# Reading PSUM banks with ScalarE first: a reordering of evacuations in a hybrid encoder trunk

## The chip, the core and the metric

One core of a Trainium2 chip runs the whole trunk as one program. Its engines are TensorE (PE, with its weight loads as PEld), VectorE (DVE), ScalarE (ACT), GpSimd (POOL) and SyncE (SP, which issues most DMAs). The metric is device time in microseconds; three runs of the kernel before give a median of 1218.54 us (1218.52 to 1218.98). The profiled execution took 1217.77 us.

## The reference, cut to what matters

```
for each of 2 layers:                      # 16 meta tokens + 1024 tokens, width 1024
  h = rms_norm(x, gain)
  f_in | q | k | v | gate = h @ w_in       # widths 512 each, gate 1024
  f_out = Re(DFT2(f_in over positions, group channels)) @ w_f       # 4 groups of 128
  q, k = rotary(rms_norm(q)), rotary(rms_norm(k))                   # 4 heads x 2 x 64
  o = (softmax(q1 k1) - lambda softmax(q2 k2)) @ v ; o = rms_norm(o)
  x = x + (concat(f_out, o) * silu(gate)) @ w_out
return x[meta tokens dropped]
```

## The kernel before

Positions lie in eight tiles of 128 tokens and a ninth of the 16 meta rows (`t == NT`). All is fp32: a matmul operand is split into a high part, rounded by ScalarE, and a low part (value minus high), mostly by VectorE, and a product is three matmuls (high x high, high x low, low x high).

A layer runs the Fourier groups first, then the projection of head 0 (`head_projection`), then `attention`. Attention is the main thread, over heads, groups of two tiles, and tiles. Between its steps it calls `fill`, which advances a generator of other TensorE work: the projections of heads 1 to 3, the output product of the Fourier half (`out_fourier`), that of the attention half (`phase_out`), and the next layer's norms.

The eight banks of PSUM are shared out in three pools. `big()` is one tile of three banks (S) for the scores; `gbank()` gives one of two banks (G) for projections and output products; `bank()` gives one of three banks (M) for transposes, for the product with V and for the Fourier maps. A bank is taken over by its next tile once every reader of the old one is done.

Within a bank the framework orders any two instructions of different engines after each other as they are written, reads too. So where the code writes a ScalarE read, a VectorE read and a ScalarE read of one bank, the third waits for the second, and the second for the first. These places matter here:

- `evacuate` (L467 to L487) empties a projection's bank: tanh of the gate (L482, ACT), gate product (L483, DVE), copy of q and k (L484), their squares (L486) and the copy of v (L487), all ACT. For the meta rows two parts are first summed from two row ranges of the bank: copy (L475, ACT) and add (L476, DVE), for each part in turn.
- `build_keys` (L576) transposes three tiles into an M bank and, for each half of the partitions, writes the scaled high part (L591, ACT) and the low part (L592, DVE).
- `build_queries` (L609) does the same with L621 (ACT) and L623 (DVE), and copies the high part to the other half of the partitions (L622, DVE; SBUF to SBUF).
- `out_tile` (L270) adds a G bank to the residual (L293, DVE); the meta rows have a second range of rows, copied by ACT (L296).
- `phase_out` (L773) prepares a tile by four transposes into a G bank (L786 to L788), read by L792 (ACT) and L793 (DVE).

`transposes` (L657) turns the softmax difference p into `ath` (L669, ACT) and `atl` (L670, DVE) over two M banks, and takes a third for the meta columns (L672). `scores` (L627) fills S (L636, L638), which one VectorE instruction (L643) empties.

The order on each engine is not written by hand. A list scheduler takes instructions by priority and by its own account of when each could start; `tc.high_priority(EVAC)` lifts evacuations, and `issue_after` holds filler behind marks in the attention. Each engine then runs its list strictly in order. The casts of the next weights (L182 ACT, L184 POOL or DVE) stand in the same lists.

Of the kernel before, what the change touches and what calls it, by code (L numbers as in the profile page):

```python
# [18 lines left out]
P = 128  # L19
# [31 lines left out]
def trunk(ctx: ExitStack, tc, x, meta, ngain, w_in, w_f, qg, kg, lq1, lk1, lq2, lk2, subg, w_out,  # L51
# [28 lines left out]
    def f(ap):  # L80
        return ap.bitcast(F32)
# [188 lines left out]
    def out_tile(yh, yl, wh, wl, xt, spare, t, wide, final=False):  # L270
# [10 lines left out]
        for group in groups:  # L281
# [8 lines left out]
            for (n, c, e), pb in zip(group, ps):  # L290
                o = xt[0:R, 512 * n + c:512 * n + e]
                with tc.high_priority(EVAC):
                    dve.tensor_tensor(o, o, pb[0:R, 0:e - c], op=ALU.add)  # L293
                    if t == NT:
                        low = spare[0:R].rearrange("p a b -> p (a b)")
                        act.copy(low, pb[2 * NMETA:2 * NMETA + R])  # L296
                        dve.tensor_tensor(o, o, low, op=ALU.add)
                if final:
                    sp.dma_start(out[0, P * t:P * t + P, 512 * n + c:512 * n + e], o)
                yield  # L300
# [156 lines left out]
    def head_projection(li, h, hT, hM, ep, wk, store, w, nxt, progress):  # L457
# [9 lines left out]
        def evacuate(t, ps, a, kv):  # L467
            nonlocal ss
            R = tile_rows(t)
            with tc.high_priority(EVAC):  # L470
                if t == NT:
                    pm = [ep.tile([P, 256], F32, tag="sq", name=nm("pm"), bufs=3) for _ in range(2)]
                    for part, u, v in ((pm[0], a, 256), (pm[1], 256, 384 if kv else 512)):
                        part = part[0:R, u % 256:(v - 1) % 256 + 1]
                        act.copy(part, ps[32:32 + R, u:v])  # L475
                        dve.tensor_tensor(part, ps[0:R, u:v], part, op=ALU.add)  # L476
                    pqk, pvg = pm[0], pm[1]
                else:
                    pqk, pvg = ps[:, 0:256], ps[:, 256:512]
                if not kv:  # L480
                    gs = ep.tile([P, P], F32, tag="gs", name=nm("gs"), bufs=2)
                    act.activation(gs[0:R], pvg[0:R, P:2 * P], AF.Tanh, scale=0.5)  # L482
                    dve.scalar_tensor_tensor(gs[0:R], gs[0:R], 1.0, pvg[0:R, P:2 * P], op0=ALU.add, op1=ALU.mult)  # L483
                act.copy(qk[0:R, t, a:256], pqk[0:R, a:256])  # L484
                sq = ep.tile([P, 256], F32, tag="sq", name=nm("sq"), bufs=3)
                act.activation(sq[0:R, a:256], pqk[0:R, a:256], AF.Square)  # L486
                act.copy(va[0:R, t, :], pvg[0:R, 0:P])  # L487
            if not kv:
                sp.dma_start(gtd[li][h][t, 0:R, :], gs[0:R])
# [67 lines left out]
    def attention(li, wk, store, fill, marks, ready, progress):  # L557
        ath = wk.tile([P, NT, 272], F32R, name="ath", bufs=1)
        atl = wk.tile([P, NT, 272], F32R, name="atl", bufs=1)
        att = wk.tile([80, 272], F32R, name="att", bufs=1)  # L560
        vt = wk.tile([80, P], F32R, name="vt", bufs=1)
        pool.memset(f(vt), 0.0)
        pool.memset(f(att), 0.0)
# [12 lines left out]
        def build_keys(h, upto, most=3):  # L576
# [3 lines left out]
            while upto > built.get(h, 0) and most > 0:  # L580
# [5 lines left out]
                for t in tiles:  # L586
                    R = tile_rows(t)
                    pe.transpose(pb[:, w:w + R], qk[0:R, t, P:256], ident[0:R, 0:R])
                    w += R
                for dst, s, o in zip(keys[h], half, half[::-1]):  # L590
                    act.activation(dst[s, a:a + w], pb[s, 0:w], AF.Copy, scale=kgc[s, li:li + 1])  # L591
                    dve.scalar_tensor_tensor(dst[o, a:a + w], pb[s, 0:w], kgc[s, li:li + 1], f(dst[s, a:a + w]),  # L592
# [4 lines left out]
        def build_values(h):  # L597
            va = store[h][1]
            vh = wk.tile([P, NT, P], F32R, tag="vh", name=nm("vh"), bufs=1)
            vl = wk.tile([P, NT, P], F32R, tag="vl", name=nm("vl"), bufs=1)  # L600
            act.copy(vh, va[:, 0:NT])
# [7 lines left out]
        def build_queries(h, gi):  # L609
# [9 lines left out]
            low = qlow[gi % 2]  # L619
            for dst, ql, s, o in ((qa, low[0], half[0], half[1]), (qb, low[1], half[1], half[0])):  # L620
                act.activation(dst[s, 0:w], pb[s, 0:w], AF.Copy, scale=qgc[s, li:li + 1])  # L621
                dve.tensor_copy(dst[o, 0:w], f(dst[s, 0:w]))  # L622
                dve.scalar_tensor_tensor(ql[s, 0:w], pb[s, 0:w], qgc[s, li:li + 1], f(dst[s, 0:w]),  # L623
                                         op0=ALU.mult, op1=ALU.subtract)
            return (qa, qb), low

# [52 lines left out]
        def values(vals, w):  # L679
# [5 lines left out]
            pe.matmul(po[:, 0:w], lhsT=vt, rhs=att[:, 0:w], start=False, stop=True)  # L685
            osb = wk.tile([P, 272], F32, tag="osb", name=nm("osb"), bufs=1)
            act.copy(osb[:, 0:w], po[:, 0:w])
            return osb

        def finish(h, gi, osb, ls):  # L690
            sets = [(0, 2, P)] + ([(2, 1, NMETA)] if len(group_tiles(gi)) > 2 else [])
            for i0, n, R in sets:
                t0 = group_tiles(gi)[i0]
                gt = wk.tile([P, 2, P], F32, tag="gt", name=nm("gt"), bufs=1)
                sp.dma_start(gt[0:R, 0:n], gtd[li][h][t0:t0 + n, 0:R, :].rearrange("t p d -> p t d"))
# [7 lines left out]
                so = sm.tile([P, 2], F32, tag="so", name=nm("so"), bufs=2)  # L703
                sqo = wk.tile([P, P], F32, tag="sqo", name=nm("sqo"), bufs=1)
                for i in range(n):
# [67 lines left out]
    def phase_out(li, nh, gb, wk, w, load, ready):  # L773
# [4 lines left out]
        def prepare(t):  # L778
# [5 lines left out]
            if t < NT and ("gy", li) in dbg:  # L784
                sp.dma_start(dbg["gy", li][:, t], ya.rearrange("p h d -> p (h d)"))
            pb = gbank()  # L786
            for k in range(4):
# [216 lines left out]
```

## Time and profile before

| | us |
|---|---|
| median of three runs | 1218.54 |
| profiled execution | 1217.77 |
| its span (first to last instruction) | 1216.0 |
| PE busy | 1164.0 (96%) |
| DVE busy | 835.8 (69%) |
| ACT busy | 643.1 (53%) |
| POOL busy | 264.7 (22%) |

The busy time of PE holds the time in which matmuls overlap or run slowly, so it says little of how full PE is; waits and the spacing of matmuls say more. The granted TensorE clock is 0.994 of full speed over the whole span. The first scores of layer 1 start at 215.9 us, those of layer 2 at 826.5 us.

### The profile page before, as it was taken

What the parts mean: (1) busy time and instruction counts of PE and PEld (TensorE: products, weight loads), DVE (VectorE), ACT (ScalarE), POOL (GpSimd) and SP (SyncE); (2) the same over time, 40 slices, a digit from 0 to 9 for tenths busy, and PEclk for the clock granted to TensorE, in tenths of its full rate; (3) what the DMA queues carried; (4) which work ended last, traced back from release to release, by engine and by line L of the source; (5) the groups of instructions that cost most, each with busy time, mean ns of one, the idle gap of its engine ahead of it and who ended that gap; (6) DMA issues with size and microseconds to landing.
All of it is one profiled execution on the core that took longest, in us unless ns stands there. A gap on an engine that the chain in (4) does not pass through costs nothing. (4 is left out here: it accounts for less than half of the span.)

```text
span 1216.0 us, 18757 instructions
## 1 busy us (share of the span) xinstructions
PE 1164.0 (96%) x6676; PEld 999.7 (82%) x6676; DVE 835.8 (69%) x1785; ACT 643.1 (53%) x1580; POOL 264.7 (22%) x239
## 2 busy tenths in 40 slices
PE   6999999999999999999999999999999999999998
PEld 5999886787787787788879999877888888878886
DVE  6352645777788788888684334458788888888963
ACT  6332324567666667566453223345576676756631
POOL 5111326023211212012012103160142122301200
PEclk9999999999999999999999999999999999999999
DMA  7420303003002004643436202120020110365353
GB/s 229 140 70 18 92 28 100 7 14 94 12 24 77 16 25 153 193 160 133 149 107 192 70 18 71 45 82 26 18 83 25 45 54 27 119 200 170 106 156 116
DMA packets 103612, 105.46 MB, mean 87 GB/s; under 512 B 11232, under 2 KB 87584, under 8 KB 103264
## 3 DMA queue, kind: packets, MB, share of 16 engines
q1 hardware_dynamic: 103104, 99.59, 26.3%
q0 software_dynamic: 416, 4.70, 1.2%
q8 instruction: 52, 0.85, 0.3%
q14 instruction: 40, 0.33, 0.1%
HBM read 74.62 MB, written 29.62 MB: 86 GB/s over the span
## 5 line engine op out<-in xcount | busy, mean ns | idle before, releaser
L548 PE MATMUL G<-wh,hT 128*128 128x512 f32 x896 | 308.7, 404 | 7.6 <-DVE pm L476 4.9
L646 ACT ACTIVATE p<-p,mx 128x1040 f32<-128x1040 f32 x136 | 158.5, 1165 | 100.2 <-DVE p L643 99.3
L548 PEld LDWEIGHTS G<-wh,hT 128*128 128x128 f32 x896 | 169.6, 190 | 47.7 <-issue 5.7
L643 DVE TENSOR_SCALAR_CACHE_REDUCE p<-S 128x1040 f32<-128x1040 f32 x136 | 167.6, 1232 | 29.6 <-PE S L638 21.8
L548 PE MATMUL G<-wl,hT 128*128 128x512 f32 x448 | 178.0, 400 | 1.1 <-POOL wl L184 0.7
L184 POOL TENSOR_TENSOR wl<-wst,wh 128x512 fp32r<-128x512 f32 x82 | 113.1, 1390 | 240.4 <-ACT wh L182 156.5
L286 PE MATMUL G<-wh,yh 128*128 128x512 f32 (+2 forms) x276 | 107.0, 400 | 4.8 <-DVE xt L293 2.6
L286 PE MATMUL G<-wl,yh 128*128 128x512 f32 (+2 forms) x276 | 105.4, 390 | 0.0
L182 ACT CAST wh<-wst 128x512 fp32r<-128x512 f32 x128 | 74.7, 619 | 57.0 <-DMA wst<-in_w_in_dram 29.0
L548 PEld LDWEIGHTS G<-wl,hT 128*128 128x128 f32 x448 | 85.6, 191 | 18.1 <-POOL wl L184 1.7
L502 POOL TENSOR_TENSOR rsq<-ss,nhalf 128x12 f32<-128x12 f32 x24 | 55.0, 2292 | 199.2 <-DVE ss L500 180.3
L352 PE MATMUL G<-hT,wh 128*128 128x384 f32 (+3 forms) x384 | 96.3, 331 | 0.0
L286 PE MATMUL G<-wh,yl 128*128 128x512 f32 (+1 forms) x260 | 92.5, 396 | 0.0
L654 DVE SCALAR_TENSOR_TENSOR p<-p,cc,p 128x1040 f32<-128x1040 f32 (+1 forms) x68 | 90.2, 1327 | 1.5
L670 DVE TENSOR_TENSOR atl<-M,ath 128x512 fp32r<-128x512 f32 x136 | 86.2, 655 | 6.9 <-ACT ath L669 6.0
L352 PE MATMUL S<-hT,wh 128*128 128x256 f32 (+3 forms) x384 | 89.1, 318 | 1.3 <-DVE sg L440 1.3
L638 PE MATMUL S<-k,ql 128*128 128x264 f32 (+3 forms) x408 | 86.9, 321 | 0.0
L669 ACT CAST ath<-M 128x512 fp32r<-128x512 f32 x136 | 72.6, 562 | 14.9 <-PE M L664 14.4
L710 POOL TENSOR_TENSOR rso<-so,nhalf 128x2 f32<-128x2 f32 (+1 forms) x36 | 27.3, 760 | 221.0 <-DVE so L708 220.7
L664 PE MATMUL M<-ident,p 128*128 128x128 f32 x544 | 73.0, 270 | 2.1 <-DVE atl L670 0.8
L684 PE MATMUL M<-ath,vh 128*128 128x256 f32 (+1 forms) x256 | 73.0, 285 | 0.8 <-DVE atl L670 0.8
L684 PE MATMUL M<-ath,vl 128*128 128x256 f32 (+1 forms) x256 | 72.6, 284 | 0.0
(194 smaller groups left out, 2504.5 us busy)
## 6 DMA issues: line engine op xcount, KB each, us to landing
wst<-in_w_in_dram SPq DMA_DIRECT2D x64, 192.0 KB, 2.8
xt<-in_x_dram SPq DMA_DIRECT2D x16, 512.0 KB, 4.1
wst<-in_w_in_dram SPq DMA_DIRECT2D x32, 256.0 KB, 4.4
wst<-in_w_out_dram SPq DMA_DIRECT2D x16, 512.0 KB, 4.2
xmid<-xt SPq DMA_DIRECT2D x16, 512.0 KB, 3.0
xt<-xmid SPq DMA_DIRECT2D x16, 512.0 KB, 4.7
tab<-in_dft_dram POOLq DMA_DIRECT2D x2, 2096.0 KB, 10.2
yfd<-sg SPq DMA_DIRECT2D x8, 520.0 KB, 2.7
```

Of the source, the lines that this page charges most:

```text
L182: act.copy(h, self.staged[q][:, j, :])
L184: eng.tensor_tensor(l, self.staged[q][:, j, :], f(h), op=ALU.subtract)
L286: pe.matmul(pb[0:m, 0:e - c], lhsT=a[:, k, 0:m], rhs=b[2 * k + n][:, c:e], start=k == 0 and i == 0, stop=k == 3 and i == n_pass - 1)
L352: pe.matmul(o, lhsT=w[k][:, c:c + P], rhs=hT[:, k, s, a:b], start=k == 0 and i == 0, stop=k == KT - 1 and i == 2)
L548: pe.matmul(pss[t][0:part.shape[-1], a:b], lhsT=part, rhs=w[k][:, a:b], start=k == 0 and i == 0, stop=k == KT - 1 and i == len(pairs) - 1)
L638: ins = pe.matmul(ps[0:R, C0 + a:C0 + b], lhsT=ql[:, qo:qo + R], rhs=kk[:, a:b], start=False, stop=True)
L643: dve.tensor_scalar(pc[0:R], ps[0:R, C0:C0 + L], -1.0, None, op0=ALU.mult, op1=ALU.min, accum_out=mx[0:R])
L646: act.activation(pc[0:R], pc[0:R], AF.Exp, bias=mx[0:R], scale=-1.0, accum_out=lc)
L654: dve.scalar_tensor_tensor(pp[0][0:R], pp[1][0:R], cc[0:R], pp[0][0:R], op0=ALU.mult, op1=ALU.add)
L664: pe.transpose(pb[:, R * j:R * j + R], pa[0:R, P * kt:P * kt + P], ident[0:R, 0:R])
L670: dve.tensor_tensor(atl[:, 4 * c:4 * c + 4, qo:qo + R], src, f(hi), op=ALU.subtract)
L684: pe.matmul(po[:, 0:w], lhsT=v[:, kt, :], rhs=a[:, kt, 0:w], start=kt == 0 and i == 0, stop=False)
```

## The change

In each bank that both engines read, the ScalarE reads are written first and the VectorE reads behind them: both copies of the meta rows before both adds, both key high parts before both low parts, both query high parts before both low parts (the copies to the other half come last), the copy of the second row range before the addition to the residual, and the gate product behind the copies of q, k and v. Two other edits stand in the same diff: five tiles of attention (`vh`, `vl`, `osb`, `gt`, `sqo`) are allocated once, where before each use took a new tile from a tag with one buffer; and in the last layer `phase_out` prepares tiles 6 and 7 in an M bank.

```diff
@@ out_tile
-                    dve.tensor_tensor(o, o, pb[0:R, 0:e - c], op=ALU.add)
                     if t == NT:
                         low = spare[0:R].rearrange("p a b -> p (a b)")
                         act.copy(low, pb[2 * NMETA:2 * NMETA + R])
+                    dve.tensor_tensor(o, o, pb[0:R, 0:e - c], op=ALU.add)
+                    if t == NT:
                         dve.tensor_tensor(o, o, low, op=ALU.add)
@@ evacuate
-                    for part, u, v in ((pm[0], a, 256), (pm[1], 256, 384 if kv else 512)):
-                        part = part[0:R, u % 256:(v - 1) % 256 + 1]
+                    parts = [(part[0:R, u % 256:(v - 1) % 256 + 1], u, v)
+                             for part, u, v in ((pm[0], a, 256), (pm[1], 256, 384 if kv else 512))]
+                    for part, u, v in parts:
                         act.copy(part, ps[32:32 + R, u:v])
+                    for part, u, v in parts:
                         dve.tensor_tensor(part, ps[0:R, u:v], part, op=ALU.add)
...
                     act.activation(gs[0:R], pvg[0:R, P:2 * P], AF.Tanh, scale=0.5)
-                    dve.scalar_tensor_tensor(gs[0:R], gs[0:R], 1.0, pvg[0:R, P:2 * P], op0=ALU.add, op1=ALU.mult)
                 act.copy(qk[0:R, t, a:256], pqk[0:R, a:256])
                 sq = ep.tile([P, 256], F32, tag="sq", name=nm("sq"), bufs=3)
                 act.activation(sq[0:R, a:256], pqk[0:R, a:256], AF.Square)
                 act.copy(va[0:R, t, :], pvg[0:R, 0:P])
+                if not kv:
+                    dve.scalar_tensor_tensor(gs[0:R], gs[0:R], 1.0, pvg[0:R, P:2 * P], op0=ALU.add, op1=ALU.mult)
@@ attention
+        vh = wk.tile([P, NT, P], F32R, name="vh", bufs=1)
+        vl = wk.tile([P, NT, P], F32R, name="vl", bufs=1)
+        osb = wk.tile([P, 272], F32, name="osb", bufs=1)
+        gt = wk.tile([P, 2, P], F32, name="gt", bufs=1)
+        sqo = wk.tile([P, P], F32, name="sqo", bufs=1)
...
+                for dst, s in zip(keys[h], half):
+                    act.activation(dst[s, a:a + w], pb[s, 0:w], AF.Copy, scale=kgc[s, li:li + 1])
                 for dst, s, o in zip(keys[h], half, half[::-1]):
-                    act.activation(dst[s, a:a + w], pb[s, 0:w], AF.Copy, scale=kgc[s, li:li + 1])
                     dve.scalar_tensor_tensor(dst[o, a:a + w], pb[s, 0:w], kgc[s, li:li + 1], f(dst[s, a:a + w]),
                                              op0=ALU.mult, op1=ALU.subtract)
...
+            for dst, ql, s, o in parts:
                 act.activation(dst[s, 0:w], pb[s, 0:w], AF.Copy, scale=qgc[s, li:li + 1])
-                dve.tensor_copy(dst[o, 0:w], f(dst[s, 0:w]))
+            for dst, ql, s, o in parts:
                 dve.scalar_tensor_tensor(ql[s, 0:w], pb[s, 0:w], qgc[s, li:li + 1], f(dst[s, 0:w]),
                                          op0=ALU.mult, op1=ALU.subtract)
+            for dst, ql, s, o in parts:
+                dve.tensor_copy(dst[o, 0:w], f(dst[s, 0:w]))
@@ phase_out
-            pb = gbank()
+            pb = bank() if last and t >= NT - 2 else gbank()
```

How this moves instructions is shown at three places. In the rows below a tile's name carries a number, which differs between the two programs for the same tile.

The first is ACT in the second layer, at the end of head 0's projection: S is the bank of tile 7, G that of the meta rows, `pm` the two parts of the meta rows, k a key's high part, `vh` the high part of V, `wh` a weight's. Before:

```order
L482 ACTIVATE gs_8611<-S_8569 128x128
L484 COPY qk_8259<-S_8569 128x256
L486 ACTIVATE sq_8615<-S_8569 128x256
L475 COPY pm_8620<-G_8570 16x128
L487 COPY va_8260<-S_8569 128x128
L591 ACTIVATE k_8672<-M_8674,kgc 64x384
L601 CAST vh_8709<-va_8260 128x1024
L591 ACTIVATE k_8672<-M_8682,kgc 64x384
L475 COPY pm_8621<-G_8570 16x128
```

and with the change:

```order
L485 ACTIVATE gs_8552<-S_8510 128x128
L486 COPY qk_8200<-S_8510 128x256
L488 ACTIVATE sq_8555<-S_8510 128x256
L489 COPY va_8201<-S_8510 128x128
L477 COPY pm_8561<-G_8511 16x128
L477 COPY pm_8562<-G_8511 16x128
L182 CAST wh_8490<-wst_8486 128x512
L182 CAST wh_8494<-wst_8486 128x512
```

The two copies of the meta rows stand next to each other, keys and values come behind them, and two weight casts that stood ahead of the tanh now follow.

The second is DVE in the second layer, where a tile's p is combined (L654, L666) while queries are built: `qa` and `qb` are the two queries, `ql` their low parts out of one M bank, `atl` the low parts of p's transposes. Before:

```order
L622 CAST qa_11016<-qa_11016 64x256
L654 SCALAR_TENSOR_TENSOR p_10962<-p_10999,cc_11010,p_10962 128x1040
L623 SCALAR_TENSOR_TENSOR ql_8648<-M_11013,qgc,qa_11016 64x256
L670 TENSOR_TENSOR atl<-M_11024,ath 128x4x128
L670 TENSOR_TENSOR atl<-M_11031,ath 128x4x128
L622 CAST qb_11017<-qb_11017 64x256
L623 SCALAR_TENSOR_TENSOR ql_8649<-M_11013,qgc,qb_11017 64x256
```

and with the change:

```order
L636 CAST qa_10932<-qa_10932 64x256
L666 SCALAR_TENSOR_TENSOR p_10878<-p_10915,cc_10926,p_10878 128x1040
L633 SCALAR_TENSOR_TENSOR ql_8594<-M_10929,qgc,qa_10932 64x256
L633 SCALAR_TENSOR_TENSOR ql_8595<-M_10929,qgc,qb_10933 64x256
L636 CAST qb_10933<-qb_10933 64x256
L682 TENSOR_TENSOR atl<-M_10940,ath 128x4x128
L682 TENSOR_TENSOR atl<-M_10947,ath 128x4x128
```

The second low part has moved ahead of the two transposes' low parts, but both still stand behind the combination of p.

The third is PE in the first layer, on the first tiles of head 1's projection, each in a G bank: tile 0 is G_2032 before and G_2037 after, tile 1 G_2125 and G_2128, and tile 2 takes the bank of tile 0. Before:

```order
L548 MATMUL G_2032<-wh_1934,hT_150 128x512
L548 MATMUL G_2032<-wl_1935,hT_150 128x512
L548 MATMUL G_2032<-wh_1934,hT_150 128x512
L548 MATMUL G_2125<-wh_1898,hT_150 128x512
L548 MATMUL G_2125<-wl_1899,hT_150 128x512
```

and with the change:

```order
L552 MATMUL G_2037<-wl_1935,hT_150 128x512
L552 MATMUL G_2037<-wh_1934,hT_150 128x512
L552 MATMUL G_2128<-wl_1935,hT_150 128x512
L552 MATMUL G_2128<-wh_1934,hT_150 128x512
L552 MATMUL G_2236<-wh_1898,hT_150 128x512
L552 MATMUL G_2236<-wl_1899,hT_150 128x512
```

Before, tile 0 ends before tile 1 begins; with the change the ends of both tiles are interleaved, and tile 2 follows two matmuls behind the last one of tile 0.

## Rows read from the trace of the kernel before

**Rows 1.** The page: span, and busy time of two engines (share, instructions).

```profile
span 1216.0 us, 18757 instructions
...
PE 1164.0 (96%) x6676; PEld 999.7 (82%) x6676; DVE 835.8 (69%) x1785; ACT 643.1 (53%) x1580; POOL 264.7 (22%) x239
```

**Rows 2.** Waits of PE: line, whom it waited for, us in total, times, longest.

```profile
PE M L672 <- DVE atl L670: 6.6, 6, 1.4
PE S L636 <- DVE p L643: 5.1, 6, 2.0
PE G L548 <- DVE pm L476: 4.9, 2, 2.6
...
PE G L548 <- ACT va L487: 2.6, 2, 2.1
...
PE S L636 <- DVE qa L622: 1.5, 2, 0.8
```

**Rows 3.** Waits of ACT, same columns.

```profile
ACT qk L484 <- DVE gs L483: 22.6, 32, 1.9
...
ACT k L591 <- DVE k L592: 5.3, 8, 1.9
ACT qb L621 <- DVE ql L623: 5.0, 8, 1.2
```

**Rows 4.** Chain that ended last, in order of time: start us, us, what.

```profile
850.00 2.83 PE M L684 x24
...
999.15 2.78 PE G L548 x12
```

**Rows 5.** Stretches: length, busy time by engine (instructions), PEclk, DMA share, GB/s.

```profile
202.60:206.10 3.50, 3.40 (x8) 2.75 (x9) 1.59 (x5) 2.85 (x10) 2.63 (x3) 0.51 0.13 36
376.70:380.10 3.40, 3.40 (x9) 2.69 (x9) 3.31 (x8) 3.22 (x7) 0.00 (x0) 0.50 0.75 205
475.70:479.10 3.40, 3.40 (x18) 3.40 (x18) 3.30 (x9) 2.74 (x6) 0.00 (x0) 0.50 0.55 146
813.60:817.00 3.40, 3.12 (x7) 2.48 (x8) 2.29 (x5) 3.12 (x8) 3.40 (x3) 0.50 0.05 13
```

**Rows 6.** Timeline, second layer, end of head 0: start, us, instruction [idle before].

```profile
810.34 0.26 ACT L475 COPY pm<-G 16x128 f32<-16x128 f32 x1
...
811.39 0.61 DVE L592 SCALAR_TENSOR_TENSOR k<-M,kgc,k 64x384 fp32r<-64x384 f32 x1 [0.44 <-ACT k L591]
...
812.80 0.26 ACT L475 COPY pm<-G 16x128 f32<-16x128 f32 x1
...
813.88 0.77 PE L548 MATMUL G<-wh,hT 128*128 128x512 f32 x1 [2.61 <-DVE pm L476]
```

**Rows 7.** Timeline, first layer, end of head 0.

```profile
202.71 0.76 PE L548 MATMUL G<-wh,hT 128*128 128x512 f32 x1 [2.34 <-DVE pm L476]
...
205.27 0.27 ACT L487 COPY va<-G 128x128 f32<-128x128 f32 x1
```

**Rows 8.** Timeline, first layer, end of head 2.

```profile
374.49 0.27 DVE L483 SCALAR_TENSOR_TENSOR gs<-gs,G 128x128 f32<-128x128 f32 x1
...
376.19 0.50 PE L548 MATMUL G<-wh,hT 128*128 128x512 f32 x1 [2.14 <-ACT va L487]
```

**Rows 9.** Timeline, second layer, queries built while p is combined.

```profile
1026.66 1.30 DVE L654 SCALAR_TENSOR_TENSOR p<-p,cc,p 128x1040 f32<-128x1040 f32 x1
...
1027.88 0.47 DVE L623 SCALAR_TENSOR_TENSOR ql<-M,qgc,qa 64x256 fp32r<-64x256 f32 x1
1028.28 1.27 DVE L670 TENSOR_TENSOR atl<-M,ath 128x512 fp32r<-128x512 f32 x2
...
1029.01 0.28 PE L672 MATMUL M<-ident,p 128*16 128x128 f32 x1 [1.39 <-DVE atl L670]
```

**Rows 10.** Timeline, last tiles of the second layer.

```profile
1196.82 0.49 PE L286 MATMUL G<-wh,yh 128*128 128x512 f32 x1 [0.25 <-DVE xt L293]
...
1203.46 0.50 PE L286 MATMUL G<-wh,yh 128*128 128x512 f32 x1 [0.34 <-DVE xt L293]
```

**Rows 11.** Costliest groups: busy us, mean ns of one, idle before.

```profile
L643 DVE TENSOR_SCALAR_CACHE_REDUCE p<-S 128x1040 f32<-128x1040 f32 x136 | 167.6, 1232 | 29.6 <-PE S L638 21.8
```

More of the change, by code (lines that the diff above doesn't have):

```diff
@@ L598, in build_values @@
             va = store[h][1]
-            vh = wk.tile([P, NT, P], F32R, tag="vh", name=nm("vh"), bufs=1)
-            vl = wk.tile([P, NT, P], F32R, tag="vl", name=nm("vl"), bufs=1)
             act.copy(vh, va[:, 0:NT])
@@ L619, in build_queries @@
             low = qlow[gi % 2]
-            for dst, ql, s, o in ((qa, low[0], half[0], half[1]), (qb, low[1], half[1], half[0])):
+            parts = ((qa, low[0], half[0], half[1]), (qb, low[1], half[1], half[0]))
+            for dst, ql, s, o in parts:
                 act.activation(dst[s, 0:w], pb[s, 0:w], AF.Copy, scale=qgc[s, li:li + 1])
-                dve.tensor_copy(dst[o, 0:w], f(dst[s, 0:w]))
+            for dst, ql, s, o in parts:
                 dve.scalar_tensor_tensor(ql[s, 0:w], pb[s, 0:w], qgc[s, li:li + 1], f(dst[s, 0:w]),
                                          op0=ALU.mult, op1=ALU.subtract)
+            for dst, ql, s, o in parts:
+                dve.tensor_copy(dst[o, 0:w], f(dst[s, 0:w]))
             return (qa, qb), low
@@ L685, in values @@
             pe.matmul(po[:, 0:w], lhsT=vt, rhs=att[:, 0:w], start=False, stop=True)
-            osb = wk.tile([P, 272], F32, tag="osb", name=nm("osb"), bufs=1)
             act.copy(osb[:, 0:w], po[:, 0:w])
@@ L693, in finish @@
                 t0 = group_tiles(gi)[i0]
-                gt = wk.tile([P, 2, P], F32, tag="gt", name=nm("gt"), bufs=1)
                 sp.dma_start(gt[0:R, 0:n], gtd[li][h][t0:t0 + n, 0:R, :].rearrange("t p d -> p t d"))
@@ L703, in finish @@
                 so = sm.tile([P, 2], F32, tag="so", name=nm("so"), bufs=2)
-                sqo = wk.tile([P, P], F32, tag="sqo", name=nm("sqo"), bufs=1)
                 for i in range(n):
```

## The prediction

> **What bounds the kernel now.** I read the page first. PE is busy for 96 % of a span of 1216.0 us, DVE for 69 %, ACT for 53 % [rows 1]. The reader is to see that only PE can be the bound, but that 96 % does not mean full: overlapping and slow matmuls count as busy. So next came the chain of waits for the pace of undisturbed matmuls. A chain step of 24 with V takes 2.83 us, which is 0.118 us a matmul, and one of 12 of a projection 2.78 us, which is 0.232 us [rows 4]. Everything that PE takes beyond that pace is what a reordering can win or lose.
>
> Then I read PE's waits by line [rows 2]. In all of them PE, which works strictly down its list, stands because a bank's old readers are not done: M for the third transposes of p (L672, 6.6 us), G behind the meta rows (4.9 us in 2 waits) and behind the copy of v (2.6 us in 2), S behind p (5.1 us in 6) and behind the query copy (1.5 us in 2). Then ACT's waits [rows 3], which are larger: 22.6 us for the gate product, 5.3 us for a key's low part, 5.0 us for a query's. They are what the change names, but ACT is off the path, so they count only where a bank that PE wants hangs on them.
>
> Last came the granted clock by stretch. [...]
>
> **Part by part: the gains.** The sum is made against the profiled execution, 1217.77 us; the median of the runs is 0.77 us higher.
>
> *Meta rows, layer 2.* The two copies are at 810.34 and 812.80 [rows 6]. Between them ACT waited, as the second is ordered behind the first addition and stood in its list behind a key's high part, which stood behind DVE's key low part (0.61 us). With the change the copies are neighbours in ACT's list (first order piece), and DVE's two additions follow. The stall of 2.61 us goes, and with it the slow stretch: 7 matmuls took 3.12 us there [rows 5], where 7 x 0.232 is 1.62, so 1.5 us. Together **4.1 us**. The bound below is 0, if the projection's bank is then late by ACT's other work.
>
> *Meta rows, layer 1.* The same place with 2.34 us [rows 7], and 8 matmuls in 3.40 us where 8 x 0.232 is 1.86, so 1.5. Together **3.8 us**, again down to 0.
>
> *Head 2 of layer 1.* PE waits 2.14 us for the copy of v, which stood behind the gate product at 374.49 [rows 8]. The 9 matmuls behind took 3.40 us instead of 2.09, another 1.3. Now v's copy is free of the gate product, but the bank is not: its last reader is now that product, and in DVE's new list it stands behind the reduction of p (mean 1.23 us [rows 11]) and a second small reduction. The bank comes free about as late. I take **0** between bounds of 0 and 3.4 us.
>
> *The third transposes of p.* 6.6 us in 6 waits [rows 2], and one is followed by the slow stretch at 475.7, where 18 matmuls took 3.40 us instead of 18 x 0.118 = 2.12: 1.3 more, 7.9 in all. At 1026.66 [rows 9] one sees why: DVE combines p for 1.30 us, then come a low part of a query (0.47) and the low parts of the transposes (1.27 in all), and L672 takes a bank of these at 1029.01. With the change the second query low part, which holds the third M bank, stands directly behind the first (second order piece); before it stood behind the transposes' low parts. That lets one of three banks go earlier, but it still stands behind the combination. Laying PE's new list out at pace, the M transposes that follow the bank's last user within 1.5 us of matmul work fall from 8 to 4; within 2.5 us they fall only from 10 to 5. Half the places, half the price: **4.0 us**, bounds 0 and 7.9.
>
> *Tiles 6 and 7 at the end.* In an M bank they no longer compete with the output product for G, where PE stands 0.25 and 0.34 us behind the residual's addition [rows 10]: **0.6 us**.
>
> *The gate product elsewhere.* ACT's 22.6 us in 32 waits [rows 3] go, since copies and squares no longer stand behind DVE. ACT is 53 % busy and PE waits for ACT's part of a G bank only twice, 2.6 us, counted above. So **0** of the rest; if ACT were late in what PE does want, up to those 22.6 us could show, but PE's waits have no row for it. The tiles allocated once had one buffer before, so they free and block as before: 0. What moves on SP and POOL in the lists are stores and casts of which none has a row among PE's waits: 0.
>
> The gains make 4.1 + 3.8 + 0 + 4.0 + 0.6 = **12.5 us**.
>
> **Part by part: the losses.** None of these is in the trace of before, so each is bounded.
>
> *Head 1 of layer 1.* PE now interleaves the ends of tiles 0 and 1, and tile 2 takes tile 0's bank two matmuls (0.46 us) behind its end (third order piece). The bank has about six ACT reads of 0.27 us [rows 7] and one DVE read of 0.27 [rows 8] to go through, 1.9 us in all. PE then waits 1.4 us. Ends: 0, if part of the reads lies in the half that ended before, and 3.4, if a slow stretch follows as above. I take **1.4**.
>
> *A key's bank.* In one place of layer 1 an M bank is taken again 0.65 us of matmul work behind its three key transposes. Its four reads, at the 0.61 us of [rows 6], take 2.4: **1.7 us**, ends 0 and 2.4.
>
> *Scores.* S is freed by one DVE instruction of 1.23 us [rows 11]. By the lists 9 of 136 scores follow their predecessor within 1.5 us of matmul work, where 7 did. One of the two new places has next to nothing in between (1.2 us), the other about 0.9 (0.3): **1.5 us**. Ends: 0 and 2 x 2.0, the longest such wait now [rows 2].
>
> *The query copy* (L622, now L636) comes last of its build, behind both low parts of 0.47 us [rows 9]. The first scores wait for it already, 1.5 us in 2 waits [rows 2]; one more low part there costs 0.47, so **0.5 us**, ends 0 and 0.9.
>
> The losses make 1.4 + 1.7 + 1.5 + 0.5 = **5.1 us**, the net is 12.5 - 5.1 = **7.4 us**: 1210.4 for a profiled execution, 1211.1 for the median, said as **1211**.
>
> **A rule weighed.** At the keys the trace shows ACT's high part waiting for DVE's low part, 5.3 us in 8 waits [rows 3], although the two read different partitions, 0 to 63 and 64 to 127. [...] The trace agrees that the order is kept by bank here; that the halves could run together no run here shows.
>
> **The rivals.**
> - *All listed stalls go and no new one comes.* 4.1 + 3.8 + 3.4 + 7.9 + 0.6 = 19.8 us, so 1198.7. For it: all of these waits end at a bank that both engines read [rows 2]. Against it: the combination of p still precedes the low parts, and the new places above are in the lists.
> - *The waits only move.* The scheduler sets the lists by its own account of times; where the bank is not free it still takes the instruction, and PE meets the same 12 us elsewhere, or the reads are written in another order and the lists keep the old one at the places that count. Then the time is 1217 to 1220. For it: gains and losses are both single places, any of which can be off. Against it: the two meta places rest on the order on ACT, which has changed as the code says.
> - *Slower: low parts in blocks hold up the freeing of S.* DVE now does a bank's low parts one behind the other: 24 key builds x 0.61 us and 32 query builds x 0.47 us more in one block, 14.6 + 15.0 = 29.7 us. Each block may stand ahead of L643, which alone frees S for the next scores. It decides from the point at which a third of it, 9.8 us, reaches PE: that eats the 7.4 us and 2.4 more. At 40 % it is 11.9 us, so 1218.5 - 7.4 + 11.9 = 1223. For it: by the lists the scores within 2.5 us of their predecessor rise from 27 to 34 of 135. Against it: PE waited for p only 5.1 us [rows 2], and DVE has 31 % idle.
>
> **How the numbers follow.** The forecast has a chance of 0.56; its own range, with half the gains or without the losses, is 1205 to 1215. All stalls gone has 0.12, waits that only move 0.17, blocks on DVE 0.15. About 0.2 % (2.4 us) is what a measurement of this kernel can tell from no change; so faster is 0.56 + 0.12 = 0.68, same 0.17, slower 0.15. The range holds the forecast and the moved waits, at its upper end the first of the slow case, 1222, and at its lower end half of the best, 1201; left out are some 0.06 below and 0.12 above.
>
> **What would show it.** PE's waits for `pm` gone, and no half clock near 203 and 814 us, while a stall and a half-clock stretch stay near 376. ACT's waits for the gate product gone with no gain of their size. The third transposes' wait at about half of 6.6 us. No idle time at the residual of the last tiles. One new wait of over 1 us on a G bank in the first layer, head 1, tile 2. I am wrong if PE's waits for p grow past 10 us, if the meta stalls come back at another reader, or if the stall at 376 goes and takes its slow stretch along.

## The result and the profile after

The changed kernel takes 1234.89 us (median of 4 runs, 1233.16 to 1236.63), the kernel before 1218.76 beside it: a ratio of 1.0124 (95 % interval 1.0104 to 1.0144). It is 16 us slower; 7.4 us less were forecast. The profiled execution took 1236.63 us.

The page of the kernel after (span; busy time, share, instructions):

```profile
span 1234.6 us, 18762 instructions
...
PE 1171.7 (95%) x6676; PEld 1006.4 (82%) x6676; DVE 840.6 (68%) x1785; ACT 640.7 (52%) x1580; POOL 260.3 (21%) x239
```

Against [rows 1] the instructions are the same in number; the span is 18.6 us longer. PE's listed waits sum to 57.8 us, 46.7 before, which is 11.1 of it. The rest is about what PE's own busy time grew by, 7.7 us; seven half-clock stretches (granted clock 0.50) stand in this execution, four in that of before. PE's waits after (line, whom it waited for, us in total, times, longest):

```profile
PE S L648 <- DVE p L655: 8.9, 11, 2.1
PE M L598 <- DVE qk L522: 5.2, 1, 5.2
PE M L676 <- DVE k L603: 4.1, 2, 2.9
PE G L552 <- DVE gs L491: 4.1, 2, 3.6
PE M L684 <- DVE ql L633: 3.9, 3, 2.1
PE M L684 <- DVE atl L682: 3.8, 3, 1.5
PE M L684 <- DVE k L603: 3.1, 2, 2.5
```

The reader is to set these beside [rows 2]. The meta rows (`pm`) and the copy of v are gone, 7.5 us. In their place stand other VectorE instructions: a key's low part (7.2 us at two lines), a query's (3.9), the gate product (4.1), and one wait of 5.2 us for the norm of the keys. Of these only the gate product is newly the last reader of its bank; the low parts were the last readers of theirs before, too. The norm's wait is for an operand, not for a bank. The waits of matmuls that write an M bank, without those at the start of a layer (L229), grew most, from 11.4 to 25.7 us, the norm's among them. ACT's waits for the gate product [rows 3] are gone, and bring nothing.

Four places of the trace after (start, us, instruction, idle before). The gate product, layer 1, third piece of the order:

```profile
205.47 2.27 POOL L506 TENSOR_TENSOR rsq<-ss,nhalf 128x12 f32<-128x12 f32 x1
...
207.57 0.29 ACT L489 COPY va<-G 128x128 f32<-128x128 f32 x1
...
207.78 1.19 DVE L508 TENSOR_TENSOR qk<-qk,rsq 128x768 f32<-128x768 f32 x1 [1.11 <-POOL rsq L506]
...
209.61 0.41 DVE L499 TENSOR_REDUCE ss<-sq 128x4 f32<-128x256 f32 x1
210.05 0.29 DVE L491 SCALAR_TENSOR_TENSOR gs<-gs,G 128x128 f32<-128x128 f32 x1
...
210.40 0.74 PE L552 MATMUL G<-wh,hT 128*128 128x512 f32 x1 [3.57 <-DVE gs L491]
```

ScalarE's last read of the bank, the copy of v, ends at 207.86 us. But the gate product stands in DVE's list behind the row norm of the keys (L508), and that waits for the power that GpSimd takes (`rsq`). The bank hangs on a chain that has nothing to do with it. A query's low parts, layer 2:

```profile
936.49 1.30 DVE L666 SCALAR_TENSOR_TENSOR p<-p,cc,p 128x1040 f32<-128x1040 f32 x1
...
937.71 0.47 DVE L633 SCALAR_TENSOR_TENSOR ql<-M,qgc,qa 64x256 fp32r<-64x256 f32 x1
938.19 0.49 DVE L633 SCALAR_TENSOR_TENSOR ql<-M,qgc,qb 64x256 fp32r<-64x256 f32 x1
...
938.83 0.27 PE L684 MATMUL M<-ident,p 128*16 128x128 f32 x1 [2.11 <-DVE ql L633]
```

DVE's list here is that of the second piece of the order. At the same transpose the kernel before waits 0.1 us. At the place of [rows 9] DVE's list is the same, and the wait is hardly changed: 1.48 us for `ql` where it was 1.39 for `atl`. A key's low parts, layer 1:

```profile
308.03 1.29 DVE L666 SCALAR_TENSOR_TENSOR p<-p,cc,p 16x1040 f32<-16x1040 f32 x1
...
309.34 1.01 DVE L603 SCALAR_TENSOR_TENSOR k<-M,kgc,k 64x272 fp32r<-64x272 f32 x2
...
310.50 1.09 PE L676 MATMUL M<-ident,p 128*128 128x128 f32 x4 [2.91 <-DVE k L603]
```

Both low parts stand behind the combination of p, and PE takes their bank with little work in between. The head of layer 2:

```profile
823.41 2.26 POOL L506 TENSOR_TENSOR rsq<-ss,nhalf 128x12 f32<-128x12 f32 x1
...
825.65 2.39 POOL L611 TENSOR_TENSOR vl<-va,vh 128x1024 fp32r<-128x1024 f32 x1
...
825.86 5.84 DVE L508 TENSOR_TENSOR qk<-qk,rsq 128x768 f32<-128x768 f32 x1
...
828.00 0.44 POOL L615 TENSOR_TENSOR vt<-va,vt 16x128 fp32r<-16x128 f32 x1
828.41 2.47 POOL L184 TENSOR_TENSOR wl<-wst,wh 128x512 fp32r<-128x512 f32 x2
...
832.88 0.90 PE L598 MATMUL M<-ident,qk 128*128 128x128 f32 x3 [5.21 <-DVE qk L522]
```

L508 takes 0.96 us in the median of its 24 times. Here it takes 5.84 and ends 0.8 us after four GpSimd instructions that run back to back, as if it did its work when they were done. In the kernel before V's low part (`vl`) stands in GpSimd's list ahead of the power (`rsq`), and the norm took 2.03 us:

```profile
812.38 2.36 POOL L602 TENSOR_TENSOR vl<-va,vh 128x1024 fp32r<-128x1024 f32 x1 [1.37 <-ACT vh L601]
...
815.93 2.27 POOL L502 TENSOR_TENSOR rsq<-ss,nhalf 128x12 f32<-128x12 f32 x1
...
818.24 2.03 DVE L504 TENSOR_TENSOR qk<-qk,rsq 128x768 f32<-128x768 f32 x1 [1.95 <-POOL rsq L502]
```

The change has turned `vl` and `rsq` round.

### The profile page after: what moved, and what is told of

The parts are those of the page before. It is cut to its first block, busy times and chain, and to the rows that moved or that the text cites. A ratio compares the mean times of both kernels' runs of the same rounds, so it can differ in the third digit from the quotient of the medians.

```text
span 1234.6 us, 18762 instructions
## 1 busy us (share of the span) xinstructions
PE 1171.7 (95%) x6676; PEld 1006.4 (82%) x6676; DVE 840.6 (68%) x1785; ACT 640.7 (52%) x1580; POOL 260.3 (21%) x239
## 4 chain that ended last, share of the span: by engine, by line
PE 68%; DVE 16%; issue 6%; ACT 4%; DMA 4%; POOL 2%; SPq 1%; POOLq 0%; DVEq 0%; ACTq 0%
PE G L552 18%; PE G L286 11%; PE G L353 7%; PE S L353 7%; PE M L696 6%; DVE p L655 4%; PE S L648 4%; PE S L650 3%; PE S L552 3%; PE M L676 3%; DVE p L666 2%; PE M L394 2%; DVE atl L682 1%; ACT p L658 1%; DMA wst<-in_w_in_dram 1%
## 5 line engine op out<-in xcount | busy, mean ns | idle before, releaser
L658 ACT ACTIVATE p<-p,mx 128x1040 f32<-128x1040 f32 x136 | 158.6, 1166 | 107.5 <-DVE p L655 106.5
L655 DVE TENSOR_SCALAR_CACHE_REDUCE p<-S 128x1040 f32<-128x1040 f32 x136 | 167.9, 1235 | 55.9 <-PE S L650 44.2
L650 PE MATMUL S<-k,ql 128*128 128x264 f32 (+3 forms) x408 | 89.4, 327 | 0.7 <-DVE ql L633 0.6
L666 DVE SCALAR_TENSOR_TENSOR p<-p,cc,p 128x1040 f32<-128x1040 f32 (+1 forms) x68 | 88.4, 1301 | 1.3
L676 PE MATMUL M<-ident,p 128*128 128x128 f32 x544 | 74.7, 273 | 6.3 <-DVE k L603 4.1
L676 PEld LDWEIGHTS M<-ident,p 128*128 128x128 f32 x544 | 62.3, 142 | 14.4 <-issue 4.8
```

What stands on the lines that cost most here:

```text
L650: ins = pe.matmul(ps[0:R, C0 + a:C0 + b], lhsT=ql[:, qo:qo + R], rhs=kk[:, a:b], start=False, stop=True)
L655: dve.tensor_scalar(pc[0:R], ps[0:R, C0:C0 + L], -1.0, None, op0=ALU.mult, op1=ALU.min, accum_out=mx[0:R])
L658: act.activation(pc[0:R], pc[0:R], AF.Exp, bias=mx[0:R], scale=-1.0, accum_out=lc)
L666: dve.scalar_tensor_tensor(pp[0][0:R], pp[1][0:R], cc[0:R], pp[0][0:R], op0=ALU.mult, op1=ALU.add)
L676: pe.transpose(pb[:, R * j:R * j + R], pa[0:R, P * kt:P * kt + P], ident[0:R, 0:R])
```

## The experiments

In all tables "us" is the median, the ratio is to the kernel before on the same chip.

**One part undone.** Each is the changed kernel with one hunk of the diff taken back; the first instead moves two operations of head 0 in layer 2 (shortened):

```diff
-            pool.tensor_tensor(vl, va[:, 0:NT], f(vh), op=ALU.subtract)     # L611; L615 (vt) alike
+            with tc.issue_after(<last key transpose>):                      # layer 2, head 0 only
+                dve.tensor_tensor(vl, va[:, 0:NT], f(vh), op=ALU.subtract)
```

> The changed kernel, but at head 0 of layer 2 the low parts of V (vl, vt) are made by VectorE behind the norm of the last keys instead of by GpSimd. In the changed kernel the row norm of qk (L508, DVE, 128x768) took 5.84 us there where it takes 0.96 elsewhere, while four GpSimd instructions ran back to back, and PE stood 5.2 us. Theory (VectorE can't start this form while GpSimd runs): that L508 falls to about 1 us, PE's wait at the last key transposes to under 1 us, the half-clock stretch there goes, and the time falls by 5 to 7 us from 1234.9, to about 1229. Rival (the instruction is slow because of its data or because ACT or DMA load the memory): L508 stays at about 5.8 us and the time stays within 1233 to 1237. The order of what follows on DVE changes too, which can move either by 3 us.

> The changed kernel with the keys' order taken back (high, low, high, low). Theory (a bank read by VectorE last comes free late, since its low parts stand behind the reductions of p on DVE): the waits of PE's transposes for the key's low part (k, 4.1 us at L676 and 3.1 us at L684) fall below 2 us, two half-clock stretches near 310 and 484 us go, and the time falls by 7 to 10 us, to 1225 to 1228. Rival (the scheduler deals the lists anew with any edit, and it is chance where PE stands): the waits for k go, others of the same sum come, and the time stays within 4 us of 1234.9.

> The changed kernel with the queries' order taken back (high, copy, low for each half). Theory (low parts late): PE's waits for the query's low part (3.9 us at L684, 0.6 at the scores) and part of those for p (8.9 us) go, so 4 to 7 us, to 1228 to 1231. Rival (dealt anew): ql waits go, others come, within 4 us of 1234.9.

> The changed kernel with the gate product back right behind the tanh. Theory (the last VectorE read late): PE's two waits for gs (4.1 us) and the half-clock stretch at 210 us behind the longer one go (5.6 us in all), the waits for the copy of v come back at most to the 2.6 us and the 1.3 us of clock of the kernel before: a net of 2 to 5 us, to 1230 to 1233. Rival (dealt anew): within 4 us of 1234.9 either way, or slower.

| changed kernel, but | us | ratio (95 %) |
|---|---|---|
| vl, vt on VectorE | 1222.96 | 1.0040 (1.0021 to 1.0058) |
| keys undone | 1223.81 | 1.0033 (1.0018 to 1.0047) |
| queries undone | 1229.93 | 1.0086 (1.0057 to 1.0114) |
| gate product undone | 1225.40 | 1.0052 (1.0035 to 1.0070) |

With V's low parts off GpSimd the norm is quick and PE's wait short:

```profile
821.37 0.94 DVE L508 TENSOR_TENSOR qk<-qk,rsq 128x768 f32<-128x768 f32 x1
...
824.45 0.60 PE L598 MATMUL M<-ident,qk 128*128 128x128 f32 x3 [0.44 <-DVE qk L522]
```

That GpSimd's work beside it lengthened the norm holds: 0.94 us where it was 5.84. But 12 us are more than the 5.2 of the wait, and more than the 5 to 7 that were expected. The lists behind that place were dealt anew, and the waits for `ql` fell from 3.9 to 1.8 us. PE's listed waits fell by only 3.9 us in all; its busy time fell by 9.7 us (1162.0 us), with three half-clock stretches where the first profile of the changed kernel has seven.

The queries came out as expected; the keys and the gate product brought more than was expected. The moved operations and the three undone parts give 12 + 11 + 5 + 9.5 = 37.5 us back, of 16 lost. They do not add up, so at least one theory was missing.

**One part alone, and the changed kernel again.** The same hunks put singly into the kernel before.

> The changed kernel once more, unedited. In the first profile of it seven half-clock stretches stand, in that of the kernel with V's low parts on VectorE three, though its layer 1 has the same lists and the same long waits; layer 1 ended 6.5 us earlier there. Theory (where the clock falls behind a wait differs from execution to execution): the waits of PE come back at the same instructions within 0.2 us each, the number of half-clock stretches does not, and L508 takes 5.8 us again. Rival (the lists fix all of it): seven stretches at the same places. The time is 1230 to 1237 by either.

> The kernel before with the gate product alone moved behind the copies. In GpSimd's list this alone puts the power of the row norm (rsq) ahead of V's low part at head 0 of layer 2, as in the changed kernel. Theory (VectorE's L508 waits out GpSimd's back-to-back work): L508 takes over 4 us at head 0 of layer 2 and PE stands over 4 us at the last key transposes; together with a wait for gs of about 3.6 us in layer 1, and the waits for the copy of v and the meta rows kept or gone as they fall, the time is 5 to 9 us above before. Rival (each edit only re-deals the lists): within 3 us of before.

> The kernel before with the keys' order alone. In GpSimd's list V's low part stays ahead of rsq in layer 2. Theory (a key's low parts in a block, behind other DVE work, free the M bank late): waits for k at the transposes of p of 4 to 7 us in all, no lock of the row norm, a time of 3 to 8 us above before. Rival (re-dealt): within 3 us of before.

> The kernel before with the queries' order alone; GpSimd's list keeps V's low part ahead of rsq in layer 2. Theory (low parts late, the copy to the other half last): waits for ql at L672 of 3 to 5 us, and the first scores 1 us later; 2 to 5 us above before. Rival (re-dealt): within 2 us of before; or faster, if the third transposes' 6.6 us of before go as the prediction had it.

> The kernel before with the meta rows' copies alone put ahead of their additions. By the prediction's first two terms PE's waits for pm (4.9 us) and two half-clock stretches go: 8 us less than before, 1211, if the rest stayed. If any new deal costs 7 to 13 us: the waits for pm go and the time lies at or above before, 1218 to 1226.

> The kernel before with the last layer's tiles 6 and 7 prepared in an M bank, nothing else; PE's list is the same up to the last 81 rows. By the prediction's term: PE's waits of 0.25 and 0.34 us at the residual go, 0.6 us less, which is below what the timing tells from nothing. Rival (the wait is passed to the next bank): no wait goes, 0.

| kernel | us | ratio (95 %) |
|---|---|---|
| changed, again | 1234.31 | 1.0116 (1.0097 to 1.0136) |
| gate product alone | 1226.30 | 1.0066 (1.0040 to 1.0092) |
| keys alone | 1232.34 | 1.0117 (1.0094 to 1.0140) |
| queries alone | 1232.79 | 1.0108 (1.0093 to 1.0123) |
| meta rows alone | 1225.97 | 1.0063 (1.0044 to 1.0081) |
| tail alone | 1217.38 | 0.9994 (0.9979 to 1.0009) |

Every edit that changes the lists early costs, and two of them cost alone nearly what all cost together: keys and queries alone lost 12 to 13 us, where 3 to 8 and 2 to 5 were expected. The meta rows are the clearest. The waits that the prediction wanted gone are nearly gone, and the kernel is slower all the same. PE's waits of that kernel, to be held against [rows 2]:

```profile
PE M L674 <- DVE atl L672: 9.3, 8, 1.7
PE S L638 <- DVE p L645: 7.9, 7, 2.6
PE S L638 <- DVE qa L624: 5.0, 3, 2.6
...
PE G L550 <- DVE pm L478: 0.7, 1, 0.7
```

`pm` fell from 4.9 to 0.7 us; `atl`, `p` and `qa`, which the edit does not touch, grew from 13.2 to 22.2. With the keys alone there is a similar stranger, 4.4 us at a projection:

```profile
PE G L548 <- ACT wh L182: 4.4, 1, 4.4
...
PE M L665 <- DVE k L593: 3.5, 2, 3.1
```

With the gate product alone GpSimd's list has the power ahead of V's low part as well, and PE waited 4.6 us for the keys' norm. But the row norm took 3.00 us, where over 4 were expected, and PE waited 1.3 us for the gate product, where about 3.6 were. The tail alone leaves all lists ahead of it as they were, and its term came out: PE's waits for the residual there are now

```profile
PE G L286 <- DVE xt L293: 2.0, 2, 1.2
```

two fewer, those of [rows 10], 0.25 + 0.34. In the timing 0.6 us is not told from nothing.

The second profile of the changed kernel has nearly the same waits (58.0 us) but four half-clock stretches where the first has seven; the matmul behind the norm's wait starts 5.3 us earlier. Two windows of the first around its waits of 2.11 and 2.91 us, and then the same two places in the second (columns as in [rows 5]), each with matmuls behind the waits; the first's longer wait is shown above, at 310.50:

```profile
220.70:224.10 3.40, 1.29 (x4) 0.63 (x4) 2.60 (x6) 0.69 (x1) 0.00 (x0) 0.50 0.00 0
...
223.52 1.21 PE L648 MATMUL S<-k,qb 128*128 128x264 f32 x3 [2.11 <-DVE p L655]
...
309.50:312.90 3.40, 2.40 (x10) 2.24 (x11) 3.23 (x8) 1.12 (x2) 0.00 (x0) 0.50 0.15 43
```

```profile
220.00:224.00 4.00, 2.33 (x12) 2.06 (x13) 2.60 (x4) 1.26 (x2) 0.00 (x0) 1.00 0.00 0
306.50:310.50 4.00, 3.62 (x20) 3.07 (x21) 3.84 (x8) 1.09 (x3) 0.00 (x0) 1.00 0.06 17
...
221.67 0.71 PE L648 MATMUL S<-k,qb 128*128 128x264 f32 x3 [2.36 <-DVE p L655]
...
306.88 0.63 PE L676 MATMUL M<-ident,p 128*128 128x128 f32 x4 [2.91 <-DVE k L603]
```

Around these stalls, of 2.1 to 2.9 us, the granted clock is 0.50 in one execution and 1.00 in the other. The four transposes behind the longer one took 1.09 us in the first and 0.63 in the second.

**New lists without new reads.** In both kernels two constants of the filler are moved a little, which changes no read but makes the scheduler deal other lists (taken place by place, 1506 to 1877 of PE's 6676 rows name other tiles than before's, 1624 with the change):

```diff
-FIRST, FILL, LAG, XHD = (8, 5), (0.96, 0.93), (7, 8), (0, 1)
+FIRST, FILL, LAG, XHD = (8, 5), (0.95, 0.92), (7, 8), (0, 1)    # or (0.97, 0.94), or (0.94, 0.95)
```

> The kernel before, no read reordered; only the two constants that set how much filler work goes between the attention's steps are changed by 0.01 (0.96 to 0.95, 0.93 to 0.92). The scheduler deals other lists: about as many rows of PE's list differ as with the change. Theory A (any new deal costs, as the lists of before are a lucky draw): 5 to 14 us above before, as each single edit. Theory B (the loss comes from the reads' new order): within 3 us of before.

> As the kernel with lower constants, but 0.97 and 0.94. Theory A (new deal): 5 to 14 us above before. Theory B (the reads' order): within 3 us.

> The changed kernel with the constants 0.95 and 0.92. GpSimd's list keeps the row norm's power ahead of V's low part in layer 2, so L508 should take over 5 us there again. Theory A (new deal alone): the loss is a draw, so the time lies 5 to 14 us above before, like before's own new deals, 1224 to 1233. Theory B (the reads' order costs by itself): 14 to 25 us above before, 1233 to 1244, that is as far above the kernel before with the same constants as the change was.

> The changed kernel with 0.97 and 0.94. Theory A: 1224 to 1233. Theory B: 1233 to 1244, about 15 us above the kernel before with the same constants.

> The kernel before with the filler constants 0.94 and 0.95, no read reordered. If a new deal costs what the first two cost: 5 to 12 us above before. If those two were chance: within 3 us of before.

> The changed kernel with 0.94 and 0.95. If the loss is that of any new deal: within 4 us of the kernel before with the same constants, to either side. If the reads' order costs by itself: 8 us or more above it. L508 takes over 5 us at head 0 of layer 2 again, as GpSimd's list has the power of the row norm ahead of V's low part.

| constants | before, us (ratio) | changed, us (ratio) | difference |
|---|---|---|---|
| 0.96, 0.93 | 1218.76 | 1234.89 (1.0124) | 16.1 |
| 0.95, 0.92 | 1228.51 (1.0069) | 1231.47 (1.0086) | 3.0 |
| 0.97, 0.94 | 1230.88 (1.0083) | 1228.67 (1.0062) | -2.2 |
| 0.94, 0.95 | 1233.46 (1.0126) | 1247.40 (1.0246) | 13.9 |

One or two hundredths in two constants cost the old reads as much as a hunk of the diff does, and the waits that grow most are some that it had. For 0.95 and 0.92 on the kernel before:

```profile
PE M L672 <- DVE atl L670: 11.3, 10, 1.8
...
PE G L548 <- ACT va L487: 4.5, 2, 2.9
```

Of these four deals of the old reads the one of before is the best; the other three lose 7 to 14.5 us against it on the same chip. Why it is the best no run shows. Over the four pairs the new reads cost 7.7 us on average, with a standard error of 4.4 (standard deviation 8.8 over the root of 4). The first pair sets the change against that best deal; over the other three the new reads cost 4.9 us, with a standard error of 4.8, which is not told from nothing.

**Reads and lists crossed.** Issue-order edges, taken from a table, hold TensorE, GpSimd and SyncE to the list of the other kernel; ScalarE and VectorE stay free to follow their reads. "Old reads" are the four orders of meta rows, gate product, keys and queries; the rest of the change stays in.

```diff
         trunk(tc, *args)
+        hold_lists(nc, tc)      # tc.add_manual_dep(ins, previous in the table, NoSync) for PE, POOL, SP
```

> The changed kernel with the lists of TensorE, GpSimd and SyncE held instruction by instruction to those of the kernel before (issue-order edges); ScalarE's and VectorE's lists follow the new order of reads. If the loss came from the newly dealt lists: 1209 to 1221, with the prediction's 1211 if its gains are real, L508 at about 2 us at most in layer 2. If the new order of reads costs by itself: 1226 to 1236, with the waits for k, ql and gs back on PE.

> The four orders of reads of the kernel before (meta rows, gate product, keys, queries), with the rest of the change and with the lists of TensorE, GpSimd and SyncE held to those of the changed kernel. If the lists cost: 1228 to 1238, with the 5 us wait of the last key transposes at head 0 of layer 2, since GpSimd's list has the power of the row norm ahead of V's low part. If the order of reads costs: 1217 to 1224.

| | lists of before | lists of the changed kernel |
|---|---|---|
| old reads | 1218.85 (the kernel before) | 1248.94 (1.0257; 1.0236 to 1.0278) |
| new reads | 1232.85 (1.0107; 1.0087 to 1.0128) | 1234.89 (1.0124; 1.0104 to 1.0144) |

Both crossings came out against "lists alone", and the second against "reads alone" too. With the three lists held the new reads cost 14 us. This isn't the reads' order by itself: of the VectorE and ScalarE instructions that no edit touches, at least 163 of 1443 and 44 of 1166 stand at other places of their lists than in the kernel before. The waits there:

```profile
PE S L648 <- DVE p L655: 8.5, 10, 2.4
PE S L648 <- DVE qa L636: 4.3, 4, 1.9
PE G L552 <- DVE gs L491: 3.7, 2, 2.0
PE M L684 <- DVE k L603: 3.1, 2, 2.5
...
PE G L286 <- ACT yh L259: 2.8, 1, 2.8
PE G L552 <- POOL wl L184: 2.6, 2, 1.8
```

`k` and `gs` read a bank that PE wants; `qa` (the copy, SBUF to SBUF, that the edit put last), `yh` and `wl` are operands that come late. `pm` has no row left. (The profiled execution, 1227.96 us, is the shortest of the five.) All of PE's waits can be sorted so: for a bank, when the releaser reads what the matmul will overwrite, or for an operand, when it makes what the matmul reads (about 1 us or less is neither).

| PE's waits, us | for banks | for operands |
|---|---|---|
| old reads, lists of before | 29.0 | 17.2 |
| new reads, lists of before | 29.3 | 26.4 |
| new reads, lists of the changed kernel | 35.3 | 21.6 |
| old reads, lists of the changed kernel | 48.3 | 22.3 |

With the lists of before held, then, the waits for banks are as long as they were in sum, and the loss stands at operands. It isn't that the banks came free late. From the last transpose into a key's bank to the end of its second low part the old reads took 5.25 us in the mean of 24 builds and the new ones 4.07; for a query's bank it was 5.18 and 3.89 us (32 builds). The new order frees these banks sooner, as it was meant to, and PE's list of before makes nothing of it. On the lists of the changed kernel the same order is worth 14 us, where the old reads free the banks about 1 us later and PE's waits for banks are 13 us longer. So the old reads are far better on their own lists. For the new reads the two lists make no difference that the intervals can tell.

## Why the prediction was wrong

- **The step that failed is the rule behind every zero of the sum, that a place not named stays as it is.** I priced about ten places; the change gave 1624 of PE's 6676 rows other tiles, and the rest was taken for zero. It is not zero: three new deals of the lists with no read reordered cost 7, 9.4 and 14.5 us against the kernel before, and the meta rows alone brought their wait down by 4.2 us while three waits that the edit does not touch grew by 9.0.
- **The first term to fail by it is the third transposes of p, "half the places, half the price: 4.0 us".** It looked for the places where PE follows the bank's last user closely in the new list, and priced them by the waits of before. The waits of all transposes of p (L664 and L672 before, L676 and L684 after, all releasers) grew from 9.8 to 17.8 us, where 4.0 less were forecast with the clock. At the third transposes alone eight waits over 0.4 us stood before; six of them stand at the same transposes after the change, each a little longer, and two new ones have come. Eleven of the 17.8 are waits for the low parts of keys and queries, 7.2 in four and 3.9 in three, where there was one of each, 0.6 and 0.5 us. In the mean these banks came free about 1 us sooner than before (4.27 and 4.08 us); what grew is the wait at a few places where PE's list takes them soon and DVE's has other work ahead of the low parts.
- **Head 1 of layer 1: the place was right, the size was not.** 1.4 us were taken from the reads' own durations; 3.57 came, since the gate product stood behind the row norm and GpSimd's power on DVE's list. That is above the upper end, 3.4, too, which was there for a slow stretch and not for this.
- **A key's bank: the place was right, the size was not.** 1.7 us with an upper end of 2.4 were given to one place of layer 1; 2.91 came there (310.50 us), and three more waits for a key's low part, 4.3 us, that were priced at nothing.
- **Head 2 of layer 1 was taken at 0, and its stall went.** No wait for a G bank over 0.2 us stands there any more, and no half-clock stretch, in either profile of the changed kernel; the prediction had named this as a sign of being wrong. With the lists of before held, its reading is borne out: PE waits 1.78 us for the gate product there.
- **"What moves on SP and POOL ... 0" failed.** Two GpSimd instructions exchanged places, and the norm of the keys took 5.84 us and ended behind four of them: 5.2 us of PE, in all five profiles of the changed kernel and of it with other constants (5.2 to 5.3 us). This was among no rival. The reason that was given for the 0 did not hold: the power is neither a store nor a cast, and GpSimd's casts have two rows of 0.7 us among PE's waits before. The norm's 2.03 us, against 0.96 in the median, stood in the trace of before.
- **Meta rows: right as a mechanism.** The 4.9 us for `pm` fell to 0.7 alone and to 0 and 0.4 in the two profiles of the whole. At the head of layer 2 a longer stall took its place (the norm, 5.2 us for 2.6); that a stall comes back at another reader the prediction named as a way to be wrong.
- **The half clock was counted as part of a stall.** 1.5 us behind each of two stalls is 3 us of the forecast, and no run shows that a stall over 2 us brings it: around the same waits, of 2.1 and 2.9 us, the granted clock was 0.50 in one execution and 1.00 in the other.
- **The order by bank** was weighed at the keys. With the new order a key's bank came free 1.2 us sooner in the mean with the lists held (4.07 us for 5.25); whether the halves could run together no run shows.
- **A misreading that cost little:** the wait for the query copy [rows 2] is for an operand, not for a bank's old readers as the prediction has it of all these rows.
- **Right:** ACT's 22.6 us for the gate product went without a gain; the tail's 0.6 us in the waits, which the timing can't show; S waits up, if by more than forecast (9.0 to 13.5 us in all, 2.0 forecast with the query copy).
- **The slower rival had the direction and named low parts in blocks on DVE, but put the loss at S.** Matmuls into M banks wait 14.3 us more, 5.2 of it for the norm, against 4.5 at S. That it is the blocks that cost is not shown: the banks came free sooner with them. The rival had a chance of 0.15.

What stays open is a division of the 16 us. The crossing gives 14 for the reads at one corner and -14 at the other; the four pairs scatter from -2 to 16. Shown are the norm's 5.2 us and that a new deal alone costs as much as most of the hunks.

## What to carry to other kernels

Where a scheduler deals the lists, a reordering is priced in two parts: what it does with the lists held, and what a new deal costs, which a change of a constant that means nothing shows on the kernel before; here that second part was a loss in three of three. A bank that comes free sooner gains only where the matmul engine's list asks for it sooner: here the same order of reads lost 14 us on one set of lists and gained 14 on the other. So sort the waits into those for banks and those for operands before blaming either. And when the order shows two GpSimd instructions exchanged beside VectorE work on SBUF, price it: here the norm took 5.84 us for 2.03.

## What the runs showed of the hardware

- VectorE's 128x768 product of two SBUF operands (0.96 us) took 5.84, 5.84, 5.85, 5.84 and 5.85 us in five profiles in which GpSimd had four instructions queued back to back, and 2.03 us in the kernel before, where it began beside a GpSimd instruction of 1.29 us; the reduction out of PSUM (L655) takes 1.24 us with or without GpSimd running. In the five traces the product ended behind all four GpSimd instructions, 0.8 us after the last of them in the one shown above.
- It doesn't always end behind all of them. With the old reads on the lists of the changed kernel, GpSimd's order was the same, yet the product took 2.20 us and ended behind one GpSimd instruction, while the next one took 1.17 us in place of 0.44. With the gate product alone it took 3.00 us, and the next one 1.99 in place of 1.25. What decides between the two no run shows.
- Around the same stall (2.11 and 2.36 us at the scores, 2.91 and 2.91 at a transpose) the granted clock was 0.50 in one execution and 1.00 in the next of the same program (seven stretches at 0.50 and four in the whole).
